# w_down's differences made once beside the up product, down's sums on VectorE, and two norm chains at the end, in a float32 transformer layer

## The chip, the cores and the metric

The kernel runs on one core of a Trainium2 chip. The metric is the device time of one execution in microseconds (us); the time before is the median of three runs, 1352.6 (1351.03 to 1353.95). Engines: PE (TensorE, matrix products), DVE (VectorE), ACT (ScalarE), POOL (GpSimd) and SP (SyncE, which only issues transfers here).

## The reference, cut to what matters

One layer of a diffusion backbone over 1024 tokens of width 1024: token mixing by windowed attention and a Fourier branch, then a gated ConvFFN of width 2816. All is float32. The change concerns the ConvFFN and the norm behind it:

```python
def conv_ffn(h, w_up, conv_w, conv_b, w_down):
    u, gate = jnp.split(h @ w_up, 2, axis=-1)
    up = jnp.pad(u, ((0, 0), (1, 1), (0, 0)))
    u = up[:, :-2] * conv_w[0] + up[:, 1:-1] * conv_w[1] + up[:, 2:] * conv_w[2] + conv_b
    return (jax.nn.silu(u) * gate) @ w_down
...
x = x + gt2 * rmsnorm(conv_ffn(h2, w_up, conv_w, conv_b, w_down), g_post2)
```

## The kernel before, in words

**Products.** A float32 product is made of three fp32r products (`mm3`, L85 to L87): each operand is split into a high half, a rounded copy made by ACT, and a low half, the difference, made by DVE (L68). On top of that the large products use Winograd's seven products in place of eight: P1 to P7, each of a combination of the stationary quarters (A11, A12, S4, A22, S1, S2, S3) with a combination of the moving quarters (`MOV`: P1 takes B11, P2 B21, P3 B22, P4 T4n, P5 T1, P6 T2, P7 T3). T1 to T4n are sums of differences of quarters: T1 = B12 - B11, T2 = B22 - T1, T3 = B22 - B12, T4n = B21 - T2.

**Steps.** The work of the ConvFFN is a list of 266 steps (`items`), one Winograd product of one pair each; the order is written out by `wino_items`. Twenty-two pairs are the up product (u0 to u21; the weights are stationary, 12 matmuls of 512 columns a step). Sixteen are down, four token pairs (d00 to d03 and so on) in each of four chunks of K tiles (`CH`: 2, 3, 3 and 3 tiles); here the gated activations are stationary and w_down moves, 6 matmuls a step in chunk 0 and 9 later. Steps 0 to 13 are written out by hand, the rest goes through `run2` (L352), which at step k first runs the hooks of that step, then `ahead(k)` (L328: loads up to 9 steps ahead, or 6 where an operand has two parts, and splits up to 4 ahead), then what is due (`flush`), then the 12, 9 or 6 matmuls. The order on each engine and on SP's queue is just the order of these calls. Down's steps begin at step 152, between the last of up's.

**Banks.** A pair's products meet in three PSUM banks X, Y and Z. P1, P6, P7 and P4 run in X one after the other, and P6, P7 and P4 can begin only when ACT has copied what is in X (`snP`). P5 and P3 run in Y: P3 can begin only when DVE has added Y and the copy of P7 (for up into `gg`, for down into `yd`).

**Up.** A tile's convolution, SiLU and gating (L1697 and on) give two gated halves. `g_sums` (L1684) makes the stationary sums S1 to S4 for down on POOL; `g_ready` (L1678) splits and stores an operand in two parts. `split_early` decides which are split here: P1, P2 and P4 of all chunks and all of chunk 0. The others are stored as one part (`rP_d`) and split in down by ACT and DVE (`hP_d`, `lP_d`). Up's own weight sums (`do_add`) run on POOL (`seng`).

**w_down.** `d_prep` (L1770) prepares a chunk's seven moving operands beside the last pair of the chunk before: 15 loads of 256 KB in five groups of three (10 in groups of two for chunk 0; B21 is loaded twice, since a difference is made in its place), differences T1, T3 and T4n on POOL and T2 on DVE, and the splits on ACT and DVE into tiles that earlier steps of PE free.

**Down's sums.** In chunk 0 the results are put into `yd`; in chunks 1 to 3 each of a pair's four results takes the PSUM bank on DVE, and three of them also the copy `snP` on POOL. In the last chunk each half row is squared on ACT and multiplied with the gate vector G2 on POOL (`d_gate`), then a norm chain of seven tiny operations and a root on ACT (`rstd_steps`), the output (L1830, DVE) and its store follow. At the end the chains of the last two rows are made as one of two columns, behind the last product, and four outputs follow.

Of the kernel before, what the change touches and what calls it, by code (L numbers as in the profile page):

```python
# [40 lines left out]
def block_kernel(ctx: ExitStack, tc: tile.TileContext, t: dict, out: bass.AP, dbg: dict):  # L41
# [1624 lines left out]
    def split_early(c, p):  # L1666
        return p in ("P1", "P2", "P4") or c == 0
# [16 lines left out]
    def g_sums(f):  # L1684
# [6 lines left out]
        def step(p, op, d, a, b):  # L1691
            return lambda: (op(d, a, b, nc.gpsimd), [(2, lambda: g_ready(f, p, d)) if early else (2, lambda: g_store(f, p, d))])[1]
# [54 lines left out]
    def d_load(c, kh, n):  # L1747
        k0, nk = CH[c]
        res = []
        for k in range(nk):  # L1750
            raw = s(f"wd{c}{kh}{n}{k}")
            r = (kh * HF + k0 + k) * P
            load(out=raw, in_=w_down[r:r + P, n * 512:(n + 1) * 512])
            res.append(raw)
        return res
# [14 lines left out]
    def d_prep(c, jl):  # L1770

        raw, nk = {}, CH[c][1]
# [2 lines left out]
        def ld(n, kh, h):
            raw[n] = d_load(c, kh, h)

        def put(o, n, k):
# [2 lines left out]
            copy(dmov[c][o][0][k], raw[n][k])  # L1781

        def put_low(o, n, k):
            sub(dmov[c][o][1][k], raw[n][k], fbits(dmov[c][o][0][k]))

        def diff(d, a, b, k, eng=None):
            if d not in raw:
                raw[d] = [s(f"d{d}{c}{i}") for i in range(nk)]
            sub(raw[d][k], raw[a][k], raw[b][k], eng)

        def split_at(i, o, n, k):
            at(i, lambda: put(o, n, k))
            at(i + 1, lambda: put_low(o, n, k))

        first = c == 0
        for i, a in zip((-4, -2, -1, 0, 2) if first else (-10, -8, -7, -5, 1),
                        (("11", 0, 0), ("21", 1, 0), ("12", 0, 1), ("22", 1, 1), ("21b", 1, 0))):
            at(i0 + i, lambda a=a: ld(*a))
        for k in range(nk):
# [6 lines left out]
            split_at(i0 + (5 if first else 2) + k, "T2", "T2", k)  # L1806
            split_at(i0 + (7, 5)[not first] + k, "T1", "11", k)
            at(i0 + 6 + k, lambda k=k: diff("T2", "21b", "T2", k, nc.gpsimd))
            split_at(i0 + (9, 8)[not first] + k, "T3", "12", k)
            split_at(i0 + 11 + k, "T4n", "T2", k)  # L1810
            split_at(i0 + 13 + k, "B22", "22", k)
# [14 lines left out]
    def d_gate(i, n):  # L1826
        mul(yd[i, n], yd[i, n], G2[n], nc.gpsimd)
# [12 lines left out]
    def down_pair(c, m):  # L1840
# [22 lines left out]
        def ev(q, pst, sn):  # L1863
# [339 lines left out]
```

## Time and profile before

| | |
|---|---|
| median of three runs | 1352.6 us |
| profiled execution | 1355.45 us, its span 1353.7 |
| busy in the span | PE 94%, DVE 76%, ACT 51%, POOL 31% |
| granted PE clock, mean | 0.986 |
| transfers | 219.42 MB, mean 162 GB/s |
| steps 29 and 152 begin at | 762.01 and 1096.70 us |
| last matmul begins at | 1343.54 us |

Rows of a timeline give the start, the duration in us (or the sum of a merged run), the engine, the line, the operation, out<-in, and in brackets how long the engine was idle before it and what ended that. Rows of the windows give for each engine its busy time in that stretch, then the granted clock of PE, the busy share of the 16 DMA engines and GB/s. Matmuls overlap: the pace of PE is the distance of their starts.

### The profile page before, as it was taken

What the parts mean: (1) busy time and instruction counts of PE and PEld (TensorE: products, weight loads), DVE (VectorE), ACT (ScalarE), POOL (GpSimd) and SP (SyncE); (2) the same over time, 40 slices, a digit from 0 to 9 for tenths busy, and PEclk for the clock granted to TensorE, in tenths of its full rate; (3) what the DMA queues carried; (4) which work ended last, traced back from release to release, by engine and by line L of the source; (5) the groups of instructions that cost most, each with busy time, mean ns of one, the idle gap of its engine ahead of it and who ended that gap; (6) DMA issues with size and microseconds to landing.
All of it is one profiled execution on the core that took longest, in us unless ns stands there. A gap on an engine that the chain in (4) does not pass through costs nothing.

```text
span 1353.7 us, 18460 instructions
## 1 busy us (share of the span) xinstructions
PE 1276.7 (94%) x5976; PEld 1027.9 (76%) x5976; DVE 1028.8 (76%) x1827; ACT 691.2 (51%) x1421; POOL 418.6 (31%) x317
## 2 busy tenths in 40 slices
PE   5899999999899999999999999999999988989896
PEld 3557877888888877778877788888888876878774
DVE  4687686975788995777889986776667687696977
ACT  5685345533667774344576544444445444443442
POOL 0000120200334333000005554445434356272754
PEclk9899999999999999999999999999999999999998
DMA  9986384514233444754213664444343569847563
GB/s 308 357 286 195 99 267 140 171 51 124 90 109 103 130 128 147 241 164 140 86 39 93 172 171 117 134 132 132 110 127 104 158 189 300 279 141 239 178 207 125
DMA packets 251125, 219.42 MB, mean 162 GB/s; under 512 B 14972, under 2 KB 204052, under 8 KB 251028
## 3 DMA queue, kind: packets, MB, share of 16 engines
q1 hardware_dynamic: 251028, 218.25, 52.2%
q8 instruction: 47, 0.77, 0.2%
q14 instruction: 50, 0.41, 0.1%
HBM read 159.20 MB, written 58.72 MB: 161 GB/s over the span
## 4 chain that ended last, share of the span: by engine, by line
PE 64%; DVE 20%; ACT 5%; DMA 5%; issue 4%; POOL 1%; SPq 0%; DVEq 0%; POOLq 0%; ACTq 0%
PE X_u L87 5%; PE X_u L85 5%; PE X_u L86 5%; PE Y_u L85 2%; PE Y_u L87 2%; PE Y_u L86 2%; PE X_g L85 2%; PE X_g L87 2%; PE X_g L86 2%; DVE p L1285 2%; PE X_d L85 2%; PE X_d L86 2%; PE X_d L87 2%; DVE pl L68 2%; DVE dT L68 2%
## 5 line engine op out<-in xcount | busy, mean ns | idle before, releaser
L68 DVE TENSOR_TENSOR lP_u<-A_u,hP_u 128x512 fp32r<-128x512 f32 x132 | 101.6, 778 | 48.0 <-ACT hP_u L303 46.4
L365 ACT COPY snP_u<-X_u 128x512 f32<-128x512 f32 x57 | 33.5, 588 | 138.3 <-PE X_u L87 130.5
L1305 POOL TENSOR_SCALAR p<-p,sm 128x640 f32<-128x640 f32 (+1 forms) x64 | 48.5, 780 | 91.6 <-PE pp L1310 40.0
L303 ACT CAST hP_u<-A_u 128x512 fp32r<-128x512 f32 x121 | 74.6, 619 | 0.1
L68 POOL TENSOR_TENSOR yd<-yd,snP_d 128x512 f32<-128x512 f32 x36 | 52.2, 1452 | 70.5 <-ACT snP_d L365 70.5
L68 POOL TENSOR_TENSOR A_u<-A_u,A_u 128x512 f32<-128x512 f32 x39 | 62.9, 1613 | 34.3 <-DVE lP_u L68 19.9
L365 ACT COPY snP_d<-X_d 128x512 f32<-128x512 f32 x48 | 28.1, 586 | 80.4 <-PE X_d L87 78.7
L68 POOL TENSOR_TENSOR A_u<-S_u,A_u 128x512 f32<-128x512 f32 x19 | 24.8, 1308 | 104.3 <-DVE lP_u L68 104.3
L80 ACT CAST ph<-pp 128x512 fp32r<-128x512 f32 x76 | 44.3, 585 | 22.5 <-PE pp L1310 21.2
L68 DVE TENSOR_TENSOR pl<-pp,ph 128x512 fp32r<-128x512 f32 x76 | 51.6, 681 | 2.5 <-ACT ph L80 2.1
L1299 ACT ACTIVATE p<-p,nm 128x640 f32<-128x640 f32 (+1 forms) x64 | 51.4, 803 | 0.7 <-DVE nm L1292 0.7
L68 DVE TENSOR_TENSOR lP_d<-rP_d,hP_d 128x384 fp32r<-128x384 f32 x48 | 42.3, 882 | 10.5 <-ACT hP_d L303 10.3
L1285 DVE CUSTOM_DVE_ANT_0 p<-ss,mask 128x640 f32<-128x640 f32 (+1 forms) x64 | 49.9, 781 | 0.0
L1310 PE MATMUL pp<-ident,p 128*128 128x128 f32 x304 | 46.7, 273 | 2.8 <-POOL p L1305 1.5
L2057 POOL MEMSET u<- 128x1 f32 x2 | 0.2, 99 | 153.4 <-DVE z L1630 149.0
L1710 DVE SCALAR_TENSOR_TENSOR tb<-u,vec,tb 128x1024 f32<-128x1024 f32 x22 | 40.9, 1860 | 6.8 <-ACT tb L1707 6.8
L1310 PEld LDWEIGHTS pp<-ident,p 128*128 128x128 f32 x304 | 37.2, 140 | 11.7 <-POOL p L1305 2.9
L68 POOL TENSOR_TENSOR S_u<-A_u,A_u 128x512 f32<-128x512 f32 x19 | 35.7, 1878 | 31.0 <-PE X_u L86 30.5
L68 POOL TENSOR_TENSOR shk<-shk,rope 128x512 f32<-128x512 f32 x2 | 3.3, 1626 | 134.8 <-DMA A_g<-in_w_in 128.9
L68 DVE TENSOR_TENSOR dB<-wd,dB 128x512 fp32r<-128x512 f32 x33 | 38.6, 1181 | 7.7 <-ACT dB L1781 7.7
L68 DVE TENSOR_TENSOR u<-Y_u,snP_u 128x512 f32<-128x512 f32 x22 | 15.2, 690 | 37.3 <-PE Y_u L87 37.3
L68 POOL TENSOR_TENSOR wd<-wd,wd 128x512 f32<-128x512 f32 x22 | 37.0, 1701 | 19.6 <-DVE dB L68 11.1
(898 smaller groups left out, 4561.2 us busy)
## 6 DMA issues: line engine op xcount, KB each, us to landing
A_u<-in_w_up SPq DMA_DIRECT2D x88, 256.0 KB, 3.9
wd<-in_w_down SPq DMA_DIRECT2D x55, 256.0 KB, 4.1
wa<-in_w_mod SPq DMA_DIRECT2D x36, 256.0 KB, 5.3
A_g<-in_w_in SPq DMA_DIRECT2D x32, 256.0 KB, 5.0
ws<-in_w_mod SPq DMA_DIRECT2D x30, 256.0 KB, 6.0
wm<-in_w_mod SPq DMA_DIRECT2D x30, 256.0 KB, 4.0
bP_d<-g_d0P SPq DMA_DIRECT2D x56, 128.0 KB, 3.2
x<-in_x SPq DMA_DIRECT2D x16, 256.0 KB, 5.7
```

The source lines that it names most:

```text
L68: return (eng or nc.vector).tensor_tensor(out=out, in0=a, in1=b, op=op)
L80: copy(hi, src)
L85: nc.tensor.matmul(ps, ah, bh, start=start, stop=False, skip_group_check=True)
L86: nc.tensor.matmul(ps, ah, bl, start=False, stop=False, skip_group_check=True)
L87: nc.tensor.matmul(ps, al, bh, start=False, stop=stop, skip_group_check=True)
L303: copy(st[j]["half", p][0], st[j][STA[p]])
L365: copy(d["s" + p], d["X"])
L1285: nc.vector.tensor_tensor_reduce(out=p_, in0=ssc[:, lo:768], in1=self.mk, op0=ALU.add, op1=ALU.max, scale=1.0, scalar=-3.0e38, accum_out=s ...
L1299: nc.scalar.activation(out=self.pt[g], in_=self.pt[g], func=AF.Exp, scale=SCALE, bias=self.m[:, g:g + 1], accum_out=self.sm[:, g:g + 1])
L1305: nc.gpsimd.tensor_scalar(out=self.pt[g], in0=self.pt[g], scalar1=self.sm[:, g:g + 1], scalar2=1.0, op0=ALU.mult, op1=ALU.mult)
L1310: nc.tensor.transpose(pp[:, g * P:(g + 1) * P], self.pt[g][:, j * P:(j + 1) * P], ident)
L1710: nc.vector.scalar_tensor_tensor(out=tb, in0=u[:, 0:1024], scalar=cw[0], in1=tb, op0=ALU.mult, op1=ALU.add)
```

## The change

- The differences of w_down are made once, beside the up product (`d_diffs`): eleven rounds, one K tile each, from step 16 on every twelve steps. A round loads four 256 KB tiles, makes T1, T3, T2 and T4n on DVE one step after another from the fourth step on, and stores each two steps later into new memory (`wt_d`).
- `d_prep` then only loads and splits: one K tile of one product per step, each loaded seven steps ahead; 21 loads of 256 KB a chunk (14 for chunk 0). No differences are left in down.
- All operands of the last chunk too are split and stored in two parts in up.
- Off POOL and onto DVE go: the sums S1 to S4 of the last two gated tiles, up's weight sums from the P1 of pair 19 on, the sums of `snP` in chunks 1 to 3, and the gates.
- At the end there are two chains. That of row 7 stands before the sum of the last product, that of row 3 behind it; one output of row 7 is made between them, and three behind the second chain.

In the rows below a tile's name ends in the pair or tile that it belongs to and a buffer's number; `h`, `l`: high and low halves; `dB`, `dT`: halves of a moving operand; `wd`: a weight tile as loaded.

On DVE at up's start, from the split for P6 of pair u12 (step 20), before:

```order
L68 TENSOR_TENSOR lP6_u12_7773<-A11_u12_7563,hP6_u12_7772 128x512
L68 TENSOR_TENSOR gf0_7698<-gf0_7698,tb0_7735 128x512
L68 TENSOR_TENSOR gg0_7648<-gg0_7648,tb0_7735 128x512
L68 TENSOR_TENSOR lP5_u12_7794<-S1_u12_7666,hP5_u12_7793 128x512
L1710 SCALAR_TENSOR_TENSOR tb11_7798<-u1_7393,vec_67,tb11_7798 128x1024
L1711 SCALAR_TENSOR_TENSOR tb11_7798<-u1_7393,vec_67,tb11_7798 128x1024
```

and now, where `wB110`, `wB120` and `wB220` are round 0's tiles:

```order
L68 TENSOR_TENSOR wB110_7720<-wB120_7722,wB110_7720 128x512
L68 TENSOR_TENSOR lP6_u12_7789<-A11_u12_7571,hP6_u12_7788 128x512
L68 TENSOR_TENSOR gf0_7706<-gf0_7706,tb0_7751 128x512
L68 TENSOR_TENSOR gg0_7656<-gg0_7656,tb0_7751 128x512
L68 TENSOR_TENSOR wB120_7722<-wB220_7724,wB120_7722 128x512
L68 TENSOR_TENSOR lP5_u12_7811<-S1_u12_7674,hP5_u12_7810 128x512
L1710 SCALAR_TENSOR_TENSOR tb11_7815<-u1_7401,vec_67,tb11_7815 128x1024
L1711 SCALAR_TENSOR_TENSOR tb11_7815<-u1_7401,vec_67,tb11_7815 128x1024
L68 TENSOR_TENSOR u1_7401<-Z_u12_7817,snP1_u12_7806 128x512
L68 TENSOR_TENSOR wB220_7724<-wB220_7724,wB110_7720 128x512
```

The differences of round 0 stand between up's own work, ahead of the convolution (`tb`).

On DVE at the turn to down, up to the sum `gg21` of up's last pair (step 153), before:

```order
L68 TENSOR_TENSOR dT201_10849<-dT200_10803,dT200_10848 128x512
L68 TENSOR_TENSOR lP4_u21_10857<-A22_u21_10464,hP4_u21_10856 128x512
L1710 SCALAR_TENSOR_TENSOR tb10_10865<-u0_7390,vec_67,tb10_10865 128x1024
L1711 SCALAR_TENSOR_TENSOR tb10_10865<-u0_7390,vec_67,tb10_10865 128x1024
L68 TENSOR_TENSOR dT201_10849<-dT201_10804,dT200_10848 128x512
L68 TENSOR_TENSOR lP3_u21_10888<-A12_u21_10462,hP3_u21_10887 128x512
L68 TENSOR_TENSOR dT101_10909<-wd0000_10623,dT100_10908 128x512
L68 TENSOR_TENSOR gf10_10812<-gf10_10812,tb10_10865 128x512
L68 TENSOR_TENSOR gg10_10752<-gg10_10752,tb10_10865 128x512
L68 TENSOR_TENSOR gg21_10935<-Y_u21_10867,snP7_u21_10906 128x512
```

and now:

```order
L68 TENSOR_TENSOR gf20_10830<-gf20_10830,gf9_10641 128x512
L68 TENSOR_TENSOR glP520_11064<-gs20_11008,ghP520_11063 128x512
L68 TENSOR_TENSOR glP720_11067<-gg9_10584,ghP720_11066 128x512
L1710 SCALAR_TENSOR_TENSOR tb10_11069<-u0_7398,vec_67,tb10_11069 128x1024
L1711 SCALAR_TENSOR_TENSOR tb10_11069<-u0_7398,vec_67,tb10_11069 128x1024
L68 TENSOR_TENSOR dT201_11049<-wdT201_10896,dT200_11048 128x512
L68 TENSOR_TENSOR lP3_u21_11093<-A12_u21_10630,hP3_u21_11092 128x512
L68 TENSOR_TENSOR glP620_11097<-gf9_10641,ghP620_11096 128x512
L68 TENSOR_TENSOR dT101_11119<-wdT100_10919,dT100_11118 128x512
L68 TENSOR_TENSOR gf10_11011<-gf10_11011,tb10_11069 128x512
L68 TENSOR_TENSOR gg10_10956<-gg10_10956,tb10_11069 128x512
L68 TENSOR_TENSOR gg21_11152<-Y_u21_11071,snP7_u21_11115 128x512
```

A sum (`gf20`) has come from POOL, and three splits for the last chunk (`glP5`, `glP7`, `glP6`) are new; the differences that fed `dT` were on POOL and DVE before and are gone.

On SP's queue in chunk 0 (steps 164 to 166), before:

```order
L1676 DMA g_d3P50_5853<-gs21_11091 128x4x128
L1676 DMA g_d3P70_5855<-gg10_10752 128x4x128
L1753 DMA wd1100_11140<-in_w_down 128x512
L1753 DMA wd1101_11142<-in_w_down 128x512
L1753 DMA wd1102_11144<-in_w_down 128x512
L236 DMA bP5_d02_11146<-g_d0P50_5820 128x256
L236 DMA bP5_d02_11146<-g_d0P51_5821 128x256
L1676 DMA g_d3P60_5854<-gf10_10812 128x4x128
L1753 DMA wd1010_11159<-in_w_down 128x512
L1753 DMA wd1011_11161<-in_w_down 128x512
L1753 DMA wd1012_11163<-in_w_down 128x512
L236 DMA bP7_d02_11165<-g_d0P70_5824 128x256
```

and now (steps 165 to 167):

```order
L1796 DMA wdB2112_11370<-in_w_down 128x512
L236 DMA bP5_d02_11372<-g_d0P50_5820 128x256
L236 DMA bP5_d02_11372<-g_d0P51_5821 128x256
L236 DMA bP7_d02_11389<-g_d0P70_5824 128x256
L236 DMA bP7_d02_11389<-g_d0P71_5825 128x256
L1796 DMA wdT210_11409<-wt_dT2_5861 128x512
L236 DMA bP1_d03_11411<-g_d0P10_5812 128x256
L236 DMA bP1_d03_11411<-g_d0P11_5813 128x256
L1676 DMA g_d3P50_5854<-ghP521_11357 128x4x128
L1676 DMA g_d3P51_5855<-glP521_11358 128x4x128
L1676 DMA g_d3P70_5858<-ghP721_11360 128x4x128
L1676 DMA g_d3P71_5859<-glP721_11361 128x4x128
```

Weight tiles (`wd`) come one per step in place of three, and the last tile's P5 and P7 are stored in two parts (`gh`, `gl`) in place of one.

The diff, without the new places' bookkeeping:

```diff
@@ split_early
-        return p in ("P1", "P2", "P4") or c == 0
+        return p in ("P1", "P2", "P4") or c in (0, len(CH) - 1)
@@ g_sums
-            return lambda: (op(d, a, b, nc.gpsimd), [(2, lambda: g_ready(f, p, d)) if early else (2, lambda: g_store(f, p, d))])[1]
+            return lambda: (op(d, a, b, nc.gpsimd if f < NF - 2 else None), [(2, lambda: g_ready(f, p, d)) if early else (2, lambda: g_store(f, p, d))])[1]
...
+    def d_diffs(r, i):
+
+        w = {}
+
+        def ld():
+            for o in ("B11", "B12", "B22", "B21"):
+                w[o] = miscF[0].tile([P, 512], F, tag="wt", name=f"w{o}{r}", bufs=4)
+                load(out=w[o], in_=d_rows(o, r))
+
+        def step(o, d, a, b):
+            sub(w[d], w[a], w[b])
+            w[o] = w[d]
+
+        at(i, ld)
+        for n, x in enumerate((("T1", "B11", "B12", "B11"), ("T3", "B12", "B22", "B12"), ("T2", "B22", "B22", "T1"),
+                               ("T4n", "B21", "B21", "T2"))):
+            at(i + 4 + n, lambda x=x: step(*x))
+            at(i + 6 + n, lambda o=x[0]: store(out=d_rows(o, r), in_=w[o]))
...
-        for k in range(nk):
-            split_at(i0 + (1 if first else -4) + k, "B11", "11", k)
-            split_at(i0 + (3 if first else -1) + k, "B21", "21", k)
-            e = 2 if first else 0
-            at(i0 + e + k, lambda k=k: diff("11", "12", "11", k, nc.gpsimd))
-            at(i0 + e + 1 + k, lambda k=k: diff("T2", "22", "11", k))
-            at(i0 + e + 2 + k, lambda k=k: diff("12", "22", "12", k, nc.gpsimd))
...
-            at(i0 + 6 + k, lambda k=k: diff("T2", "21b", "T2", k, nc.gpsimd))
...
+        for n, o in enumerate(OPS):
+            for k in range(nk):
+                i = i0 + (1 + 2 * n if c == 0 else 3 * n - 6 if n < 2 else 3 * n - 5) + k
+                at(i - 7, lambda o=o, k=k: ld(o, k))
+                at(i, lambda o=o, k=k: put(o, k))
+                at(i + 1, lambda o=o, k=k: put_low(o, k))
@@ d_gate, down_pair
-        mul(yd[i, n], yd[i, n], G2[n], nc.gpsimd)
+        mul(yd[i, n], yd[i, n], G2[n])
...
-                add(y, y, sn, nc.gpsimd)
+                add(y, y, sn)
...
+    for r in range(HF):
+        d_diffs(r, 16 + 12 * r)
...
+    at(pos[NF - 3, "P1"], lambda: seng.__setitem__(0, nc.vector))
@@ the end
+        evac_last = due[M].pop()
+        flush(M)
         d_square(i1, 0)
         d_gate(i1, 0)
-        flush(M)
+        rs1 = rstd_steps(ssd[:, i1, :], f"d{i1}")
+        rs1[0]()
+        rs1[1]()
+        assert not evac_last()
...
         d_square(i0, 1)
-        y01 = s("y01")
-        mul(y01, yd[i0, 1], G2[1], nc.gpsimd)
-        v, sq, r, n1 = (tiny(f"{n}dl", 2, 8) for n in ("v", "sq", "r", "n1"))
...
-        for i, n in ((i1, 1), (i1, 0), (i0, 0), (i0, 1)):
...
+        d_out(i1, 1, rs1[2])
+        d_store(i1, 1)
+        rs0 = rstd_steps(ssd[:, i0, :], f"d{i0}")
+        rs0[0]()
+        d_gate(i0, 1)
+        rs0[1]()
+        d_out(i0, 0, rs0[2])
+        d_store(i0, 0)
+        d_out(i0, 1, rs0[2])
+        d_store(i0, 1)
+        d_out(i1, 0, rs1[2])
+        d_store(i1, 0)
```

More of the change, by code (lines that the diff above doesn't have):

```diff
@@ L1745, in block_kernel, with d_rows @@
     dmov = {c: {} for c in range(len(CH))}
-    def d_load(c, kh, n):
-        k0, nk = CH[c]
-        res = []
-        for k in range(nk):
[L1751 to L1755, printed above, removed]
+    wt_d = {o: dscr(f"wt_d{o}", [HF * P, 512]) for o in ("T1", "T2", "T3", "T4n")}
+    PLACE = {"B11": (0, 0), "B12": (0, 1), "B21": (1, 0), "B22": (1, 1)}
+    def d_rows(o, r):
+        if o in wt_d:
+            return wt_d[o][r * P:(r + 1) * P, :]
+        kh, n = PLACE[o]
+        return w_down[(kh * HF + r) * P:(kh * HF + r + 1) * P, n * 512:(n + 1) * 512]
+    def d_diffs(r, i):
[12 more added lines that the diff above has]
+            at(i + 6 + n, lambda o=x[0]: store(out=d_rows(o, r), in_=w[o]))
     def d_place(c, o):
@@ L1770, in d_prep, with ld, put @@
     def d_prep(c, jl):
[L1772 removed]
+        raw, (k0, nk) = {}, CH[c]
         i0 = pos[jl, "P1"]
[L1775 to L1778 removed]
+        def ld(o, k):
+            raw[o, k] = s(f"wd{o}{c}{k}")
+            load(out=raw[o, k], in_=d_rows(o, k0 + k))
+        def put(o, k):
             if k == 0:
                 d_place(c, o)
[L1781 to L1784 removed]
@@ L1786, in diff @@
[L1786 to L1798, printed above, removed]
@@ L1799, in d_prep @@
[L1799 to L1811 removed]
+            copy(dmov[c][o][0][k], raw[o, k])
```

13 lines of the change are left out of this document (2 added, 11 removed).

## The prediction

> **What bounds the kernel now.** I read the page first, then the windows by stage, the waits of the matmul engine (PE) in the last stretch, and the timelines of PE, DVE and POOL around each wait.
>
> ```profile
> PE 1276.7 (94%) x5976; PEld 1027.9 (76%) x5976; DVE 1028.8 (76%) x1827; ACT 691.2 (51%) x1421; POOL 418.6 (31%) x317
> ```
>
> PE is the bound on average, but 94% is a mean over stages. The windows (columns: length, busy time of PE, PEld, DVE, ACT, POOL, granted clock, DMA share, GB/s) show where the missing time lies:
>
> ```profile
> 800.00:1080.00 280.00, 280.00 (x1237) 231.86 (x1236) 186.61 (x230) 129.92 (x212) 124.13 (x86) 1.00 0.47 133
> 1080.00:1112.00 32.00, 28.14 (x118) 22.80 (x117) 29.79 (x32) 15.05 (x26) 17.35 (x10) 0.95 0.57 160
> 1112.00:1180.00 68.00, 63.81 (x272) 51.70 (x271) 47.85 (x60) 32.40 (x60) 28.21 (x19) 0.97 0.92 298
> ...
> 1200.00:1220.00 20.00, 15.59 (x68) 12.24 (x67) 20.00 (x22) 7.57 (x15) 13.86 (x9) 1.00 0.41 120
> ```
>
> In the up product PE never stops: 280 us / 1237 matmuls = 0.226 us each, so a step (one product of one pair) of 12 matmuls is 2.72 us, of 6 (down, first chunk) 1.36, of 9 (later chunks) 2.04. Around the turn to down (1080 to 1112) and at a chunk's change (1200 to 1220) PE stops while DVE is full, 20.00 of 20; between them (1112 to 1180) the transfers are, at a share of 0.92. The waits of PE from 1100 to the end (us in total, times, longest):
>
> ```profile
> PE Y_d L85 <- DVE yd L68: 9.2, 5, 2.6
> PE X_d L85 <- ACT snP_d L365: 6.2, 3, 2.5
> PE Y_u L85 <- DVE gg L68: 3.9, 1, 3.9
> PE Z_d L85 <- DMA bP_d<-g_d0P: 2.3, 1, 2.3
> PE X_d L85 <- DMA bP_d<-g_d0P: 0.7, 1, 0.7
> ```
>
> That is 22.3 us: 19.3 for DVE and ACT, 3.0 for transfers. A stop costs more than its wait. The first matmuls start late: below, 2.22 and 0.33 us between starts for 1.83 of wait, so 2.22 + 0.33 - 2 x 0.226 - 1.83 = 0.27 more.
>
> ```profile
> 1203.42 0.39 PE L87 MATMUL Y_d<-dT,lP_d 128*128 128x512 f32 x1
> 1205.64 0.50 PE L85 MATMUL X_d<-dT,hP_d 128*128 128x512 f32 x1 [1.83 <-ACT snP_d L365]
> 1205.97 0.39 PE L86 MATMUL X_d<-dT,hP_d 128*128 128x512 f32 x1
> ```
>
> And after some stops the granted clock falls:
>
> ```profile
> 1105.00:1110.00 5.00, 3.83 (x10) 3.02 (x11) 4.11 (x7) 2.08 (x4) 0.00 (x0) 0.66 0.47 145
> 1140.00:1145.00 5.00, 5.00 (x15) 3.96 (x16) 5.00 (x6) 0.97 (x2) 3.90 (x3) 0.66 0.78 231
> 1310.00:1315.00 5.00, 5.00 (x16) 3.90 (x17) 3.89 (x7) 2.05 (x6) 4.03 (x3) 0.66 1.05 384
> 1335.00:1340.00 5.00, 2.47 (x8) 1.85 (x8) 4.56 (x10) 0.68 (x2) 2.45 (x2) 0.87 0.28 105
> 1340.00:1345.00 5.00, 3.93 (x12) 2.30 (x11) 2.48 (x4) 1.65 (x5) 2.27 (x2) 0.79 0.28 105
> ```
>
> At 0.66 a slice of 5 us loses 0.34 x 5 = 1.7 us; three of these and 0.7 + 1.0 at the end make 6.8 us.
>
> Why DVE is full: its durations near 1081 and near 1090, and POOL's (two answers):
>
> ```profile
> 1081.77 0.68 DVE L68 TENSOR_TENSOR dB<-wd,dB 128x512 fp32r<-128x512 f32 x1
> 1082.37 0.69 DVE L68 TENSOR_TENSOR lP_u<-S_u,hP_u 128x512 fp32r<-128x512 f32 x1
> ...
> 1089.47 1.77 DVE L68 TENSOR_TENSOR dB<-wd,dB 128x512 fp32r<-128x512 f32 x1
> 1091.16 1.78 DVE L68 TENSOR_TENSOR dT<-wd,wd 128x512 f32<-128x512 f32 x1
> 1092.87 0.68 DVE L68 TENSOR_TENSOR u<-Y_u,snP_u 128x512 f32<-128x512 f32 x1
> ```
>
> ```profile
> 1089.07 1.62 POOL L68 TENSOR_TENSOR gg<-gf,gg 128x512 f32<-128x512 f32 x1
> 1090.65 1.74 POOL L68 TENSOR_TENSOR wd<-wd,wd 128x512 f32<-128x512 f32 x1
> ```
>
> The same dB difference takes 0.68 (0.60 from start to start) with POOL idle and 1.77 with POOL working; the sum from PSUM, with one SBUF operand, stays at 0.68. One POOL operation thus takes about 1.1 us away from DVE beside its own time, and each later chunk's weights bring nine of them close together.
>
> **The change part by part.** *The turn to down.* The sums of the last two tiles, up's last weight sums and chunk 0's differences leave POOL; the last chunk's P3, P5, P6 and P7 get their splits here, on ACT and DVE. From the first weight split (step 147) to the sum gg of the last up pair (step 153) DVE's new order holds 25 short operations and two of 1024 columns.
>
> ```profile
> 1114.44 1.28 DVE L1710 SCALAR_TENSOR_TENSOR tb<-u,vec,tb 128x1024 f32<-128x1024 f32 x1 [0.45 <-ACT tb L1707]
> ```
>
> That is 25 x 0.60 + 2 x 1.28 = 17.6 us, against PE's 5 x 2.72 + 2 x 1.36 + 2.72 = 19.0 until the product that needs gg. The wait of 3.9 goes (bounds 0 to 2 left, if DVE comes late), and its slow clock, 1.7.
>
> *Chunks 1 to 3.* POOL's differences go, its 36 sums and its gates go to DVE, and of the splits in the last chunk 16 go. Per pair of chunks 1 and 2 DVE now has 7 sums and 5.25 weight splits at 0.60 and four low halves of 384 columns, at most 0.60 each: 9.8 us in 7 x 2.04 = 14.3 of PE. In chunk 3 it has 7 sums, 4 gates and 4 outputs at about 0.65, and two norm chains at some 1.5: 12.8 of 14.3. So the five waits for yd (9.2) go, and two of the three for snP_d (3.7), where ACT stood behind a weight that waited for DVE. The third, on the last pair, stays in part: its P4 needs snP_d right after P7, behind a root on ACT; I keep 1.4 of 2.5, which takes 1.1 off. Eight waits gone save 8 x 0.27 = 2.2 beside, and the slow clock at 1310 (1.7) goes and half of that at the end (0.8). Should DVE stay late there, 5 us of this are kept.
>
> *Transfers in chunk 0.* What they cost, from a stretch of stores only in pieces of 512 B, and one mostly of loads:
>
> ```profile
> 764.50:770.60 6.10, 6.10 (x29) 5.05 (x28) 6.10 (x8) 3.33 (x5) 2.89 (x3) 1.00 1.07 299
> ...
> 1130.20:1140.00 9.80, 6.82 (x29) 4.99 (x27) 6.87 (x8) 5.23 (x10) 5.90 (x4) 1.00 1.08 375
> ```
>
> 256 KB are 0.262 MB / (299 / 1.07) = 0.94 us stored and 0.262 / (375 / 1.08) = 0.755 us loaded. By the order of its queue SP issues in steps 150 to 183: before 18 such stores, 15 loads of 256 KB, 16 of 192 and 52 of 128, 56.9 us; now 26, 24, 16 and 52, 71.2 us. PE needs 4 x 2.72 + 28 x 1.36 + 2 x 2.04 = 53.0 us there, and with six steps of lead (12.2) less some 2 for landing the queue has 63. So it falls 8 us behind, unless bursts matter more: before it fit by 6 and still made PE wait 3.0, since nine weight loads and eight stores stood in a row. Now the weights come one per step. I take 7 us of wait for 3.0, +4.0, and leave the clock loss at 1140 as it is; ends -3 (spread well) and +9. The Trainium skill, DMA: Bandwidth & Descriptors, Specifications, puts line rate at transfers of 512 B and more; by that a store would cost the load's 0.755, the new queue 66 us and the wait some 3. The row of 0.94 decides against it. In chunk 3 the operands come split: a pair loads 2.7 MB in place of 1.9, beside x1 and the output; at most 13.7 us in 14.3, hidden by the lead.
>
> *The differences in up.* Eleven rounds of four products on DVE, 8 loads and stores of 256 KB on SP; DVE has 93 us idle from 800 to 1080, so 44 x 0.60 fit; cost 0 there. Not at up's start, where DVE has a backlog (DVE's rows, PE's row, and PE's only wait for gg before 1100):
>
> ```profile
> 747.85 1.01 DVE L68 TENSOR_TENSOR lP_u<-A_u,hP_u 128x512 fp32r<-128x512 f32 x1 [0.97 <-ACT hP_u L303]
> ...
> 777.90 0.68 DVE L68 TENSOR_TENSOR gg<-Y_u,snP_u 128x512 f32<-128x512 f32 x1
> ```
>
> ```profile
> 781.18 0.39 PE L85 MATMUL Y_u<-B22a,hP_u 128*128 128x512 f32 x1
> ```
>
> ```profile
> PE Y_u L85 <- DVE gg L68: 1.7, 1, 1.7
> ```
>
> Round 0 stands before that wait: 4 x 0.60 less the 0.97 idle makes it 1.5 longer. Three operations of round 1 stand before the next gg, which has 781.18 - 778.58 = 2.6 us to spare: 1.8 to 5.1 us, by POOL; I take 0.8. Together +2.3 (0 to 6, with a slow clock).
>
> *The end.* Of PE's last matmul, DVE and the last output:
>
> ```profile
> 1343.54 0.40 PE L87 MATMUL Y_d<-dB,lP_d 128*128 128x512 f32 x1
> ```
>
> ```profile
> 1343.97 0.69 DVE L68 TENSOR_TENSOR yd<-yd,Y_d 128x512 f32<-128x512 f32 x1 [2.08 <-PE Y_d L87]
> ...
> 1350.00 0.75 DVE L1830 SCALAR_TENSOR_TENSOR yd<-y,rdl,xf 128x512 f32<-128x512 f32 x1
> ```
>
> One output less lies behind the root (0.7), and no POOL gate beside the sums (some 0.7). Against it the first chain now stands on DVE before the last sum: two sums, two gates, seven small operations and a trip to ACT, some 4 us in a product of 2.04. I count 0 (-1.4 to +2).
>
> **The sum**: waits -3.9 - 9.2 - 3.7 - 1.1, late starts -2.2, clock -1.7 - 1.7 - 0.8, transfers +4.0, start of up +2.3: -18.0. The profiled execution took 1355.45 us (its span of 1353.7 and 1.75 around it), 2.85 over the runs' median of 1352.6. I take the sum off the median: 1334.6.
>
> **Rivals.** *Transfers become the bound* (chance 0.17): the queue's 12 us of wait and a second slow clock: 1334.6 + 5 + 2 = 1341.6. For it: 1.08 of DMA share already. Against: 12 more stores and loads lie where PE stood at gg. *Spread loads suffice* (0.13): no wait for transfers, no clock loss, up's start free: 1334.6 - 7 - 1.7 - 2.3 = 1323.6. *DVE is the bound after all* (0.04): its operations keep some 1.2 us without POOL; 12.25 x 1.2 = 14.7 us and the low halves against 14.3, so the waits stay: about 1352. The Trainium skill, Perfetto Trace Analysis, Optimizing Scalar/DVE Operations, would offload a saturated DVE, even to GpSimd, though it doubts that for the port they share; the rows of 0.68 and 1.77 side with its doubt. *Slower* (0.06): the rounds in up meet POOL each time; four operations at 1.70 are 6.8 us, 4.2 over the 2.6 to spare, and PE waits 4.2 in half of the eleven: 23 us, 1357.6. It decides from 18.0 / 11 = 1.6 us per round on. Against it: DVE's idle third there.
>
> **How the numbers follow.** My sum has 0.60. The range takes the second rival and most of the first: 1323 to 1345. A change below 0.2% (2.7 us) can't be told from none here. Faster by more: 0.60 + 0.17 + 0.13 = 0.90; within: 0.04; slower: 0.06.
>
> **What would show it.** Right: no POOL row after 1080; DVE's two-operand differences at 0.68 in down; no PE wait for gg or yd near the chunks' changes; the largest PE wait left is for bP_d or hP_d between steps 170 and 183. Wrong: PE waits for gg between 800 and 1080, DVE full in down, or waits for transfers over 12 us.

## The result, and the profile after

The changed kernel takes 1344.7 us (median of 4 runs, 1343.69 to 1345.93), the kernel before 1352.14 beside it: a ratio of 0.9944, 95% interval 0.9927 to 0.9961. In a second comparison it was 1343.11 against 1353.49, 0.9922 (0.9908 to 0.9937). So it is faster by 7 to 10 us; 18 were forecast, and 1344.7 lies at the very end of the range. The profiled execution took 1345.93 us, its span 1344.2, 9.5 less than before's.

The page, the windows by stage and PE's waits from 1100 to the end, in the changed kernel:

```profile
PE 1275.7 (95%) x5976; PEld 1024.8 (76%) x5976; DVE 1037.4 (77%) x1929; ACT 691.6 (51%) x1418; POOL 272.0 (20%) x216
```

```profile
800.00:1080.00 280.00, 280.00 (x1237) 231.91 (x1236) 233.08 (x281) 134.16 (x220) 118.88 (x78) 1.00 0.66 196
1080.00:1112.00 32.00, 31.82 (x140) 26.02 (x139) 27.82 (x42) 19.54 (x34) 0.00 (x0) 1.00 0.80 239
1112.00:1180.00 68.00, 60.74 (x253) 47.35 (x252) 42.63 (x68) 33.23 (x60) 0.00 (x0) 0.97 1.01 324
1200.00:1220.00 20.00, 20.00 (x90) 16.57 (x89) 15.09 (x26) 8.44 (x17) 0.00 (x0) 1.00 0.69 215
```

```profile
PE X_d L85 <- ACT snP_d L365: 3.4, 1, 3.4
PE Z_d L85 <- DMA bP_d<-g_d0P: 2.8, 1, 2.8
PE Y_d L85 <- DVE yd L68: 2.0, 3, 1.3
PE X_d L85 <- DMA bP_d<-g_d0P: 2.0, 3, 1.2
PE Y_d L85 <- DMA bP_d<-g_d0P: 1.2, 1, 1.2
PE Y_u L85 <- DVE gg L68: 0.2, 1, 0.2
```

The turn (1080 to 1112) and the chunk's change (1200 to 1220) are full now: PE 31.82 of 32 and 20.00 of 20, POOL at nothing, VectorE at 15.09 of 20. VectorE took 46 us more from 800 to 1080 (233.08 for 186.61) without one stop of PE there. What is left stands in chunk 0 (waits for `bP_d`, 6.0 us), at one `yd` and at the last `snP_d`, which grew from 2.5 to 3.4. From 1080 on no two-operand operation of VectorE on 512 columns takes longer than 0.7 us; two of the turn:

```profile
1091.61 0.68 DVE L68 TENSOR_TENSOR gs<-gg,gg 128x512 f32<-128x512 f32 x1
1092.94 0.68 DVE L68 TENSOR_TENSOR dB<-wdB,dB 128x512 fp32r<-128x512 f32 x1
```

**Place by place.** The steps are the same 266 in every kernel here, so the start of a step can be set against that of the same step before: 764.51 for 762.01 at step 29, 1107.78 for 1106.16 at step 155. The table gives how much later (+) or earlier (-) each stretch of the profiled execution ends than it did before, by the starts of steps 28, 154, 161, 169, 206, 248, 263 and 265; the last column runs from step 265 to the end of the span.

```
                        to 28  up to 154  turn 161  to 169  chunk 0, 206  changes, 248  chunk 3, 263  to 265   end   sum
forecast                  0.0       +2.3      -5.9    -1.5          +4.0          -9.9          -5.1    -1.9   0.0  -18.0
changed                  +0.4       +4.9      -5.2    +0.1          +4.1         -10.0          -3.8    +0.6  -0.6   -9.5
changed, again           +0.5       +3.2      -5.2    +0.1          +3.1         -10.0          -3.7    +0.7  -0.8  -12.2
rounds from step 28      -1.4       +1.7      -5.3    +0.1          +4.6         -10.0          -3.7    +1.2  -0.5  -13.4
last chunk not split     -1.9       +3.2      -5.7     0.0          -3.0         -10.0          -2.7    +1.7  -0.6  -19.1
gates and roots later    -3.0       +3.8      -5.3    +0.1          +4.3         -10.0          -5.1    -1.8  -0.8  -17.8
last sums later           0.0       +3.8      -5.3    +0.1          -2.8         -10.0          -3.8    +1.5  -0.4  -16.8
sums, gates on POOL      -1.4       +4.2      -5.3    +0.1          +3.5         -10.0          -2.6    -0.6  -0.5  -12.6
turn on POOL             -2.3       +3.2      -5.5    +0.1          +3.5         -10.0          -3.7    +1.1  -0.4  -14.1
one chain at the end     -1.2       +4.9      -5.3    +0.1          +3.7         -10.0          -3.7    +0.6  -0.6  -11.4
differences alone        -1.3       +3.8      -5.7     0.0          -2.5         -10.0          -1.4    +0.2   0.0  -16.9
all but differences      -3.2        0.0      +0.8    +0.1          +3.3          -9.6          -3.7    +1.2  -0.4  -11.6
three edits              -1.3        0.0      -5.3    +0.1          -2.8         -10.0          -5.1    -1.8  -0.7  -26.9
and two orders           -0.4        0.0      -5.2    -1.1          -0.7         -10.0          -5.1    -1.9  +0.2  -24.2
six more stores later    -0.1        0.0      -5.2    -1.2          -5.2         -10.0          -5.1    -1.8  -0.8  -29.4
no last split, 3 edits   -1.1        0.0      -5.7    -1.2          -1.1         -10.0          -5.1    -1.8  -0.8  -26.8
```

The first column is the same work in all but for round 0 of the differences, which stands ahead of step 28 where rounds begin at step 16; the rows with it (-3.0 to +0.5) and without it (-3.2 to -0.1) overlap, so it shows how much two executions differ by themselves: 3.8 us between the ends. Where nothing was changed at their place, the turn, the changes and chunk 3 repeat to 0.1 us, the last two steps to 0.9, up's start and chunk 0 (a slow clock, transfers) to 1.5 to 1.7.

### The profile page after: what moved, and what is told of

Its sections match the earlier page's. It is cut to its first block, busy times and chain, and to the rows that moved or that the text cites. A ratio compares the mean times of both kernels' runs of the same rounds, so it can differ in the third digit from the quotient of the medians.

```text
span 1344.2 us, 18657 instructions
## 1 busy us (share of the span) xinstructions
PE 1275.7 (95%) x5976; PEld 1024.8 (76%) x5976; DVE 1037.4 (77%) x1929; ACT 691.6 (51%) x1418; POOL 272.0 (20%) x216
## 5 line engine op out<-in xcount | busy, mean ns | idle before, releaser
L68 DVE TENSOR_TENSOR lP_u<-A_u,hP_u 128x512 fp32r<-128x512 f32 x132 | 108.6, 829 | 30.0 <-ACT hP_u L303 28.4
L68 POOL TENSOR_TENSOR A_u<-A_u,A_u 128x512 f32<-128x512 f32 x35 | 57.9, 1655 | 24.7 <-DVE lP_u L68 11.9
L68 DVE TENSOR_TENSOR yd<-yd,snP_d 128x512 f32<-128x512 f32 x36 | 24.8, 690 | 32.6 <-ACT snP_d L365 32.6
L1710 DVE SCALAR_TENSOR_TENSOR tb<-u,vec,tb 128x1024 f32<-128x1024 f32 x22 | 41.9, 1904 | 3.6 <-ACT tb L1707 3.6
L68 DVE TENSOR_TENSOR lP_g<-A_g,hP_g 128x512 fp32r<-128x512 f32 x48 | 33.3, 699 | 9.8 <-ACT hP_g L80 9.8
L1281 PE MATMUL ss<-kst,qs 128*128 128x384 f32 (+1 forms) x128 | 36.5, 366 | 1.3 <-DVE mx L1285 0.8
L1711 DVE SCALAR_TENSOR_TENSOR tb<-u,vec,tb 128x1024 f32<-128x1024 f32 x22 | 36.4, 1656 | 0.9
L68 DVE TENSOR_TENSOR wB<-wB,wB 128x512 f32<-128x512 f32 x44 | 35.7, 810 | 0.0
L1321 PE MATMUL po<-pl,vst 128*128 128x512 f32 x76 | 31.3, 412 | 2.7 <-DVE pl L68 2.2
L1737 ACT COPY gf<-X_u 128x512 f32<-128x512 f32 x22 | 12.9, 586 | 38.4 <-PE X_u L87 37.8
```

Of the source, the lines that this page charges most:

```text
L68: return (eng or nc.vector).tensor_tensor(out=out, in0=a, in1=b, op=op)
L1710: nc.vector.scalar_tensor_tensor(out=tb, in0=u[:, 0:1024], scalar=cw[0], in1=tb, op0=ALU.mult, op1=ALU.add)
```

## The experiments

**The changed kernel again**, beside three others.

> The changed kernel itself, on the same chip as the three kernels that run with it, since the kernel before varies between 1351 and 1356 from one chip to another. 0.9944 of the time before, 1344.7 to 1346.5.

Measured: 1343.11 us, 0.9922 (0.9908 to 0.9937), a little better than expected.

**The start of up.** The edit:

```diff
-        d_diffs(r, 16 + 12 * r)
+        d_diffs(r, 28 + 11 * r)
```

> Round r starts at step 28 + 11r in place of 16 + 12r, so that no difference stands on VectorE before the product that waits 3.8 us for gg at 764.5; the same 44 differences and 88 transfers are made. Theory (a backlog on VectorE at up's start, and a slow clock behind a stop that it makes too long): that wait is back at about 1.7 us, matmuls keep 0.227 us from start to start behind it, and everything from step 30 on comes some 4.5 us earlier; about 1340.2. Rival (the product of those steps only arrives earlier at chunk 0, where the transfers are the bound by their own time): step 152 comes 4.5 us earlier, but waits for bP_d grow by as much, and the time stays at 1344 to 1345.

Measured: 1341.33 us, ratio 0.9903 (0.9886 to 0.992). What the rounds had done is seen in VectorE's rows of the changed kernel ahead of the product of step 29, and PE's there:

```profile
758.10 3.49 DVE L68 TENSOR_TENSOR lP_u<-A_u,hP_u 128x512 fp32r<-128x512 f32 x2
761.50 1.75 DVE L68 TENSOR_TENSOR gf<-gf,tb 128x512 f32<-128x512 f32 x1
763.17 0.68 DVE L68 TENSOR_TENSOR gg<-gg,tb 128x512 f32<-128x512 f32 x1
763.78 0.68 DVE L68 TENSOR_TENSOR gg<-Y_u,snP_u 128x512 f32<-128x512 f32 x1
```

```profile
764.51 0.80 PE L85 MATMUL Y_u<-B22a,hP_u 128*128 128x512 f32 x1 [3.81 <-DVE gg L68]
765.10 0.63 PE L86 MATMUL Y_u<-B22a,hP_u 128*128 128x512 f32 x1
765.53 0.63 PE L87 MATMUL Y_u<-B22a,lP_u 128*128 128x512 f32 x1
```

Before, `gf` took 0.68 and began at 760.07. Moved back by four differences, it now falls beside a POOL operation,

```profile
760.99 1.72 POOL L68 TENSOR_TENSOR gf<-gf,gf 128x512 f32<-128x512 f32 x1
```

and takes 1.75. So the wait is 3.81 for 1.73, and then matmuls are 0.43 apart in place of 0.227, 2.8 us of loss. Without the round the wait is 1.7 and the clock stays:

```profile
760.59 0.50 PE L85 MATMUL Y_u<-B22a,hP_u 128*128 128x512 f32 x1 [1.73 <-DVE gg L68]
760.93 0.40 PE L86 MATMUL Y_u<-B22a,hP_u 128*128 128x512 f32 x1
761.17 0.39 PE L87 MATMUL Y_u<-B22a,lP_u 128*128 128x512 f32 x1
```

But round 0 now stood before the next `gg`, and PE waited 1.4 us there (step 43). So a part of the price was kept, +1.7 for +3.2 to +4.9. The times alone do not show the gain (0.9903 lies near the changed kernel's second ratio, 0.9922, and the intervals overlap); the columns do. The rival, that chunk 0 eats the gain, falls: chunk 0 is +4.6 for +4.1 and +3.1, and its waits for `bP_d` are 7.1 us for 6.0, not 4.5 more. With rounds from step 40 on (below) the column is 0.0, which shows the whole price of those two rounds: 3 to 5 us.

**Chunk 0's transfers**, from two sides. In the first the last chunk's splits go back to down; in the second only the last tile's sums, with their eight stores, come later:

```diff
-        return p in ("P1", "P2", "P4") or c in (0, len(CH) - 1)
+        return p in ("P1", "P2", "P4") or c == 0
```

> The last chunk's P5, P6, P7 and P3 are stored as one part again and split in the last chunk, as before the change; nothing else is undone. Theory (bytes in chunk 0 make its 5.9 us of waits): eight stores of 256 KB fewer near the turn and chunk 0, 8 x 0.94 = 7.5 us of queue, so waits for bP_d fall to 2 or less; chunk 3 gets 16 splits back on ACT and VectorE (four low halves a pair, 2.2 us, on 12.8 of 14.3) and gives some 2 us back; about 1342.5. Rival 1 (VectorE cannot take the splits in chunk 3): waits for yd and snP_d of 5 us and more there, 1346 or more. Rival 2 (chunk 0 waits by the order of its queue and not by bytes): waits for bP_d stay near 6, 1346 to 1347.

```diff
-                rest = [(4, lambda: g_ready(f, "P2", gt[0])), (4, lambda: g_ready(f, "P4", gt[1])), (5, lambda: g_sums(f))]
+                rest = [(4, lambda: g_ready(f, "P2", gt[0])), (4, lambda: g_ready(f, "P4", gt[1])), (5 if f < NF - 1 else 36, lambda: g_sums(f))]
```

> The sums S1 to S4 of the last gated tile, with their four splits and eight stores, come 31 steps later, in chunk 1, where transfers have room; nothing is left out. Theory (bytes in chunk 0): 8 x 0.94 = 7.5 us of queue fewer before step 183, waits for bP_d fall from 5.9 us to 1.5 or less, with the slow clock at 1140; 4 to 6 us less, about 1340. Rival 1 (a late landing of single loads by the order of the queue): waits stay at 4 or more, 1343 or more. Rival 2 (VectorE's room in chunk 1): new waits of PE for yd or snP_d near 1205, 1343 or more, with chunk 0's waits gone.

Measured: 1338.82 us (0.9883, 0.9866 to 0.9901) and 1338.03 (0.9877, 0.9859 to 0.9896). Chunk 0 turns from +4.1 to -3.0 and -2.8, and the waits for `bP_d` from 6.0 us to 0.8 and 0.7, so the rivals (the queue's order, VectorE's room) fall. The stretch from 1130 to 1160, in the changed kernel and with the last sums later:

```profile
1130.00:1160.00 30.00, 24.01 (x93) 17.29 (x92) 13.79 (x23) 12.23 (x23) 0.00 (x0) 0.94 1.01 321
```

```profile
1130.00:1160.00 30.00, 28.80 (x123) 22.22 (x122) 18.23 (x30) 15.97 (x31) 0.00 (x0) 1.00 0.99 331
```

The share of the transfers is 1 in both, and PE makes 123 matmuls for 93: what differs is that eight stores no longer stand among the loads that it needs. Eight stores at the prediction's 0.94 are 7.5 us; the swing from +3.1 or +4.1 to -2.8 is 5.9 to 6.9. The Trainium skill, DMA: Bandwidth & Descriptors, Specifications, puts line rate at transfers of 512 B and more. Priced by that as loads, at the load's 0.755 us, the eight stores are an estimated 6.0, so this swing does not decide between the two prices. In chunk 3 the splits back in down cost 1.0 us (-2.7 for -3.8), less than the 2 expected.

**VectorE behind ACT in chunk 3.** Each gate one step later, each root behind the copy of the next product:

```diff
-                d_gate(i, n)
+                gate = [(1 if i != NT - 1 else 0, lambda: d_gate(i, n) and None)]
...
-                return [(1, rs[0]), (2, lambda: [rs[1](), d_out(i, 0, rs[2]), d_out(i, 1, rs[2])] and None),
+                return gate + [(2, rs[0]), (3, lambda: [rs[1](), d_out(i, 0, rs[2]), d_out(i, 1, rs[2])] and None),
...
```

> In the last chunk each gate product stands one step later on VectorE (behind the next sum, so that ACT's square of the same tile is done), and each chain's root one step later, behind the copy of P7. Theory (VectorE waits for ACT's square before each gate, 0.8 us a time, and the root in turn holds ACT's copy snP_d): the last wait of PE for snP_d falls from 3.4 to about 1.2 us, the slow clock behind it is shorter; 2 to 3 us less, about 1342. Rival (the outputs and chains only move behind the last matmul): the last matmul begins 2 us earlier, but the stretch behind it grows from 9.3 to 11 or more, and the time stays within 0.7 us of 1344.7.

Measured: 1338.09 us, 0.9881 (0.9866 to 0.9896). The rows that led here are VectorE's in the last pairs of the changed kernel, and ACT's and PE's at the last stop:

```profile
1318.56 0.68 DVE L68 TENSOR_TENSOR yd<-yd,Z_d 128x512 f32<-128x512 f32 x1
1320.09 0.69 DVE L68 TENSOR_TENSOR yd<-yd,G 128x512 f32<-128x512 f32 x1 [0.85 <-ACT jd L1824]
1320.70 0.68 DVE L68 TENSOR_TENSOR yd<-yd,X_d 128x512 f32<-128x512 f32 x1
1322.17 0.69 DVE L68 TENSOR_TENSOR yd<-yd,G 128x512 f32<-128x512 f32 x1 [0.79 <-ACT jd L1824]
```

```profile
1328.34 0.20 ACT L144 ACTIVATE sqd<-vd 128x1 f32<-128x1 f32 x1 [3.78 <-DVE vd L143]
1328.45 0.57 ACT L365 COPY snP_d<-X_d 128x512 f32<-128x512 f32 x1
```

```profile
1329.07 0.50 PE L85 MATMUL X_d<-dT4n,hP_d 128*128 128x512 f32 x1 [3.38 <-ACT snP_d L365]
```

A gate (`G`) overwrites the tile `yd` that ACT is squaring (into `jd`), so VectorE stands 0.8 to 0.9 us before eight of the sixteen gates; this makes the chain's sum `vd` late, the root waits for it, and the copy behind the root too. With both later, ACT copies as soon as PE is done:

```profile
1320.05 0.58 ACT L365 COPY snP_d<-X_d 128x512 f32<-128x512 f32 x1 [2.21 <-PE X_d L87]
1320.65 0.20 ACT L144 ACTIVATE sqd<-vd 128x1 f32<-128x1 f32 x1
```

PE's waits from 1280 to the end are then

```profile
PE Y_d L85 <- DVE yd L68: 1.1, 1, 1.1
PE X_d L85 <- ACT snP_d L365: 0.7, 1, 0.7
```

The wait for the last `snP_d` is 0.68 us for 3.38, those at steps 253 and 260 are gone, one of 1.15 for the last `yd` has come, and chunk 3 and the last two steps give 1.3 and 2.4 us. The end did not grow, so the rival falls. The edit moves gates and roots at once; what each is worth was not measured apart.

**What the move off GpSimd is worth.** Two undoings, the sums of `snP` and the gates in one, the turn's sums in the other:

```diff
-                add(y, y, sn)
+                add(y, y, sn, nc.gpsimd)
...
-        mul(yd[i, n], yd[i, n], G2[n])
+        mul(yd[i, n], yd[i, n], G2[n], nc.gpsimd)
```

> The sums of snP in chunks 1 to 3 and the gates go back to GpSimd, from the changed kernel; the weights' differences stay in up. Theory (the stops at the chunks' changes came from the nine differences of a chunk, which stood close together, and not from GpSimd's 12 sums a chunk): no wait of PE for yd or snP_d near the changes to chunks 2 and 3; each sum takes 1.1 us from VectorE in place of 0.6, 1.5 us more of VectorE in 14.3 a pair, hidden; in chunk 3 VectorE no longer waits for ACT's squares (3.2 us a pair) but loses 3.5; within 2 us of the changed kernel on the same chip. Rival (any operation of GpSimd beside VectorE stops PE there): the waits at the changes return, 5 to 10 us slower than the changed kernel.

```diff
-            return lambda: (op(d, a, b, nc.gpsimd if f < NF - 2 else None), [(2, lambda: g_ready(f, p, d)) if early else (2, lambda: g_store(f, p, d))])[1]
+            return lambda: (op(d, a, b, nc.gpsimd), [(2, lambda: g_ready(f, p, d)) if early else (2, lambda: g_store(f, p, d))])[1]
...
-    at(pos[NF - 3, "P1"], lambda: seng.__setitem__(0, nc.vector))
```

> The sums S1 to S4 of the last two gated tiles and up's last weight sums go back to GpSimd, from the changed kernel. Theory (GpSimd beside VectorE at the turn made the stop of 3.9 us): eight to sixteen operations of GpSimd take 1.1 us each from VectorE, and the wait for gg at step 155 is back at 2 to 4 us, with the slow clock behind it; 2 to 5 us slower than the changed kernel. Rival (chunk 0's differences alone made that stop, and they are gone): the wait stays at 0.2, no change.

Measured: 1342.93 us (0.9925, 0.9912 to 0.9939) and 1343.46 (0.9924, 0.9911 to 0.9937), both the same as the changed kernel on that chip (0.9922). The changes stay at -10.0 with the sums on POOL. Chunk 3 is 1.1 us worse (-2.6) and the last two steps 1.2 better (-0.6; the last wait for `snP_d` is 2.0 us for 3.4), so the two sides cancel. At the turn my theory falls and the rival holds: -5.5, with no wait at all.

**The two halves of the change.** The kernel before with `d_diffs`, the new `d_prep` and its tiles alone; and the changed kernel with `d_load` and `d_prep` of before, without the rounds.

> The kernel before with the weights' differences alone: made beside up (step 16 on, every 12), kept in memory, one tile per step in down. Splits, sums, gates, GpSimd's other work and the end stay as before. Theory (the differences of a chunk, close together on GpSimd and VectorE, were what stopped PE at the chunks' changes and at the turn): changes to chunks 2 and 3 -9.9, turn -5, chunk 0 without the eight more stores -2, start of up +3 to +5; ratio to before about 0.990. Rival (GpSimd's sums and gates beside VectorE stop PE too): waits for yd or snP_d of 2 us stay near the changes, ratio 0.995 or more.

> The changed kernel with the weights' differences back in down, on GpSimd and VectorE, and without the rounds in up; splits of the last chunk, sums and gates on VectorE and the end stay as changed. Theory (as for the kernel with the differences alone, from the other side): the waits at the changes stay at 1.5 to 2.6 us each, up's start is as before, chunk 0 gets the eight stores (+3 to +6); ratio to before 0.998 to 1.004. Rival (the sums moved off GpSimd are what cures the changes): 0.993 or less.

Measured: 1338.6 us (0.989, 0.9877 to 0.9902) and 1345.57 (0.9941, 0.9928 to 0.9955). The first is as expected, and faster than the whole change (0.9944 and 0.9922): what else was changed costs 4 to 7 us on balance. By place that gains 2.3 us in chunk 3 and loses 5.6 to 6.6 in chunk 0. The second kernel came out otherwise: I had expected the stops at the changes to stay, and they went (-9.6 for -10.0). The window of a chunk's change, first with the differences alone, then with all but them:

```profile
1200.00:1220.00 20.00, 20.00 (x90) 16.57 (x89) 14.97 (x21) 10.50 (x21) 6.73 (x5) 1.00 0.73 225
```

```profile
1200.00:1220.00 20.00, 20.00 (x89) 16.54 (x89) 20.00 (x32) 10.27 (x21) 5.01 (x3) 1.00 0.56 177
```

Before, this window had VectorE and POOL at 20.00 and 13.86 and PE at 15.59. Either half takes enough off POOL: the first leaves VectorE 5 us of room, the second leaves it full but just not late. By the prediction's price a sum that moves costs VectorE 0.6 and gives back 1.1; the six that stand on POOL between 1188 and the second stop (1216.69) give 3.0 of the 4.4 us of stops per change. That sum is argued, not measured apart. The Trainium skill, Perfetto Trace Analysis, Optimizing Scalar/DVE Operations, doubts that work moved between these two engines helps, for the port they share. Here both happen: with the differences beside them the twelve sums a chunk are worth moving (0.3 us of stops at the two changes for 8.8), without them the move is worth nothing (-10.0 either way). The turn is decided by the differences too: PE's wait at step 155 in the kernel with all but them is

```profile
PE Y_u L85 <- DVE gg L68: 4.6, 1, 4.6
```

and 0.2 or none in every kernel without chunk 0's differences.

**The end.** The tail of before in the changed kernel (one chain of two columns, four outputs behind it):

> The changed kernel with the end of before: one chain of two columns behind the last product, and four outputs behind it; the gate of the last output on GpSimd. Theory (the two chains cost and save alike): within 1 us of the changed kernel, 0.992. Rival (three outputs in place of four behind the root are worth their 0.7 us each): 1.5 to 2 us slower, 0.9935.

Measured: 1344.05 us, 0.9929 (0.9916 to 0.9941), which holds both forecasts (0.992 and 0.9935); the columns decide. The end is -0.6 with one chain, and -0.6 and -0.8 with two. Two chains are worth no more than one, within 0.3 us.

**The three edits together**: rounds from step 40 on, every ten steps; gates and roots later; the last sums later.

> Rounds from step 40 on, one every ten steps; gates and roots one step later; the last tile's sums 31 steps later. Theory (three causes in three places, which add up): start of up -3 to -5, chunk 0 -7, end -4; 14 to 16 us less than the changed kernel on the same chip, ratio to before about 0.983, 1331. Rival 1 (PE that comes earlier meets the same transfers): waits for bP_d of 4 us and more are back in chunk 0, ratio 0.987 to 0.988, as the best of the single edits. Rival 2 (the rounds, closer together, meet VectorE's full stretch at the turn): the wait for gg at step 155 grows to 2 us and more, with a slow clock.

> The kernel with three edits once more, for comparison on one chip; ratio 0.9805 to 0.9836.

Measured: 1329.35 us, 0.9821 (0.9805 to 0.9836), and once more 1328.41, 0.9816 (0.9802 to 0.9829). That is 13.8 us under the changed kernel on that chip (14 to 16 expected), and the three causes add up: 0.0, -2.8, and -5.1 with -1.8.

**What is left then.** At step 162 a wait of 1.27 us was still there. VectorE's rows in the changed kernel show why:

```profile
1114.55 1.28 DVE L1710 SCALAR_TENSOR_TENSOR tb<-u,vec,tb 128x1024 f32<-128x1024 f32 x1 [0.46 <-ACT tb L1707]
...
1118.29 0.69 DVE L68 TENSOR_TENSOR gf<-gf,tb 128x512 f32<-128x512 f32 x1
1118.90 0.68 DVE L68 TENSOR_TENSOR gg<-gg,tb 128x512 f32<-128x512 f32 x1
1119.50 0.68 DVE L68 TENSOR_TENSOR yd<-Y_d,snP_d 128x512 f32<-128x512 f32 x1
```

The sum that PE needs (`yd`) stands behind the last tile's gating, which follows ACT's SiLU. The gating now goes behind that sum, and the outputs of a row behind the sums of their step (beside the three edits):

```diff
-            return [(1, conv), (2, silu), (3, gate)] + rest
+            return [(1, conv), (2, silu), (3, gate if f < NF - 1 else lambda: [(0, gate)])] + rest
...
+                return gate + [(2, rs[0]), (3, lambda: [rs[1]()] and [(0, lambda: [d_out(i, 0, rs[2]), d_out(i, 1, rs[2])] and None)]),
...
```

> As the kernel with three edits together, and besides the last gated tile's gating stands behind the sum that PE waits for at step 162, and the outputs of a row stand behind the sums of its step. Theory (both waits are VectorE standing behind work of ACT, not a full VectorE): the wait of 1.27 us at step 162 and that of 1.1 us before the last product go; 2 to 3 us less than with three edits, ratio 0.980. Rival (transfers hold chunk 0: what PE gains at step 162 it waits for at step 174 again): only the end's part, 0.5 to 1 us.

Measured: 1331.37 us, 0.9833 (0.982 to 0.9845): not better than three edits. The wait at step 162 went (-1.1), and chunk 0 gave it back (-0.7 for -2.8), as the rival said; the wait before the last product stayed (1.0 us for 1.1), and the outputs moved made the end 0.9 longer (+0.2 for -0.7); they were dropped. So the queue's bytes were next, and two kernels asked about them: one moves six more stores out of chunk 0 (14 in all), the other does without the last chunk's splits.

> As the kernel with three edits, with the last tile's gating behind the sum for step 162, and the six other stores of the last two gated tiles (P1 of one, P2 and P4 of the other, in two parts each) 28 to 34 steps later, so that 14 stores have left chunk 0. Theory (what reordering won at step 162 was lost to bytes of the queue): waits for bP_d and hP_d before step 184 at 1 us or less in all, step 184 some 1.5 to 2.5 us earlier than with three edits; ratio about 0.9805. Rival (those stores come back as a wait in chunk 1, where the share of the transfers is already 0.8 to 0.9): step 184 earlier, but waits for hP_d in chunk 1; no difference from the three edits.

> Rounds from step 40 on, gates and roots one step later, gating of the last tile behind the sum for step 162, and the last chunk split in down as before the change (its twelve more stores are not made). Theory (the stores' cost is in chunk 0 alone, and the splits save about 1 us in chunk 3): 0 to 2 us slower than with three edits. Rival (with the gates later VectorE has room in chunk 3, and the splits in up are worth nothing): equal or faster.

Measured: 1324.7 us, 0.9783 (0.977 to 0.9797), and 1328.97, 0.9817 (0.9804 to 0.9831). With 14 stores moved, chunk 0 is -5.2, and PE's waits from 1100 to the end are 2.0 us in all:

```profile
PE Y_d L85 <- DVE yd L68: 1.1, 1, 1.1
PE X_d L85 <- ACT snP_d L365: 0.7, 1, 0.7
PE Y_u L85 <- DVE gg L68: 0.2, 1, 0.2
```

There is no wait in chunk 1, so that rival falls. This is the fastest kernel here, 29 us under the kernel before; the changed one is 7 to 10 under it. Without the last splits, and with the gates later, the time is that of the three edits, and chunk 3 and the last two steps stay at -5.1 and -1.8: the splits made in up are worth nothing once VectorE does not wait for ACT.

## Why the prediction was half right

- **Turn** (-5.9, measured -5.2; -5.7 without the new splits) and **changes of chunk** (-9.9, measured -10.0): right in size. The reason given was too wide. The turn was stopped by chunk 0's differences alone, not by the sums of the last tiles; the changes are cured by either half of the change, so it pays twice for the same 10 us.
- **Transfers in chunk 0** (+4.0, measured +4.1 and +3.1): right in sum; the waits for `bP_d` were 6.0 us, not 7, and what stood around them made up for it. It is the net of two: without the stores there, the stretch is 2.5 to 3.0 us shorter than before, and the stores cost 5.6 to 7.1.
- **Start of up** (+2.3, measured +4.9 and +3.2): the term that was mis-sized. The four differences were priced at their length. They also moved `gf` beside a POOL operation (1.1 more), and the longer stop brought a slow clock of 1.4 to 2.8 us, which stood only in the range's upper end. The 0.8 for round 1 was nothing, since PE came later.
- **Step 162** (-1.5, measured +0.1), **chunk 3** (-5.1, measured -3.8) and **the last two steps** (-1.9, measured +0.6): here the step failed that turns a sum into a wait. The prediction added up VectorE's operations (12.8 of 14.3 us a pair) and concluded "so the five waits for yd (9.2) go"; of the last `snP_d` it kept 1.4 us of 2.5, and 3.4 were there. What was left of these waits was not a full VectorE, but VectorE standing behind ACT in its own order: at step 162 in both kernels alike (1.21 and 1.27 us), and in chunk 3 anew, since the gates, once on POOL, made POOL wait for the squares and now make VectorE wait. The gates were counted at their length (0.65) without the 0.8 before half of them. With the same work on VectorE and only gates and roots later, the two places give -5.1 and -1.8, where -5.1 and -1.9 were forecast; for the last two steps this is partly chance, as a wait of 1.15 for the last `yd` stands in the place of what was kept for `snP_d`. 5.4 of the 8.5 us that are missing in the profiled execution are here, 2.6 at up's start.
- **Clock**: the loss behind step 253 went in every kernel (1.6 us between the starts of steps 253 and 255), also with the differences alone, where the stop before it stayed at 2.4 us. So its gain was real but not for the reason given; that at the end did not go (0.66 from 1330 to 1335).
- **The end** (0, measured -0.6): right, and not through the chains, as one chain gives the same.
- **Rivals**: transfers as the bound came out nearest in time (1341.6), but by another way; PE waited 6 us for them, not 12. VectorE as the bound and slow rounds in up are excluded: PE has no wait from 800 to 1080 and is full at the changes. Of the signs named, POOL's silence behind 1080, the 0.68 and the changes came as said; the largest wait left was to be for an operand in chunk 0, and is for `gg` (3.8) and `snP_d` (3.4).

## What to carry to other kernels

A sum of busy time says whether an engine can keep up, not whether it does: for every operation that is moved onto an engine, ask what it waits for there, since all that is queued behind it waits too. When two edits aim at the same stop, price each alone; the second may be worth nothing and still bring its own costs. Work put into a stretch with room on average goes behind that stretch's narrow places, and stores that nobody needs soon go behind the transfers that somebody waits for.

## What had not been expected of the hardware

- After much the same stop at step 29 (3.2 to 3.8 us) the slow clock took 1.4 to 1.6 us in six of the profiled executions and 2.7 to 2.8 in three; after 1.7 us of wait there was none. A stop of 2.16 us at step 253 before was followed by a slow clock (0.66), one of 2.42 at the same step, in the kernel with the differences alone, by none (its granted clock is the last figure but two of the row). What decides it was not found.

```profile
1294.00:1299.00 5.00, 4.64 (x20) 3.86 (x21) 4.41 (x8) 2.40 (x7) 3.53 (x3) 1.00 1.02 369
```

- The share of the transfers does not tell whether PE waits. The fastest kernel has the same rate around chunk 0 as the changed one, whose PE waits 6 us for transfers there, and its own PE never stops:

```profile
1105.00:1165.00 60.00, 60.00 (x265) 49.32 (x264) 42.91 (x69) 32.71 (x60) 0.00 (x0) 1.00 0.99 323
```

against, in the changed kernel,

```profile
1112.00:1172.00 60.00, 52.74 (x218) 40.74 (x217) 39.08 (x63) 32.23 (x58) 0.00 (x0) 0.97 1.01 323
```
